# A gate product on rows without the norm: filling the seam between attention and the second MLP of a two-layer trunk

## The chip, the cores and the metric

The kernel runs on one core of a Trainium2 chip. The metric is the device time of one execution in microseconds (us). Times shown are medians of several executions; the profile comes from one execution of its own, whose time is given beside its span.

## The reference, cut to what matters

The trunk has two layers over 256 latent tokens (and 256 context tokens) of width 2048. What matters here is the end of layer 1: attention's output product, the norm in front of the MLP, and the MLP's first two products.

```python
h = h + ml[:, 2] * y_lat                       # y_lat = attention(...) @ w_o
u = modulate(rms_norm(h, norm2_g[i]), ml[:, 3], ml[:, 4])    # x * (1 + scale) + shift
gp = u @ w_gate                                # D_FF = 5504 = 43 column tiles of 128
gte = conv of width 3 over tokens (gp) + conv_b
h = h + ml[:, 5] * ((silu(gte) * (u @ w_up)) @ w_down)
return rms_norm(h, final_norm_g)
```

`rms_norm` multiplies a token's row by one number, rstd = (mean of squares + eps) ** -0.5. With the norm's gain and (1 + scale) folded into one factor M per channel, u = h * M * rstd + shift. So u @ w = rstd * ((h * M) @ w) + shift @ w, where rstd belongs to the token and shift @ w to the output channel.

## The kernel before

Channels lie on partitions: `hl` is 16 tiles (k = 0 to 15) of 128 channels by 256 tokens. Every product is in float32r, with weights and rows each split in a high part (a cast on ACT, line 148, `activation` or copy for rows) and a low part (value minus high part, a subtraction on DVE or POOL, line 150 for weights). A column tile of a layer-1 MLP product is 16 matmuls with the high weights against high and low rows side by side (512 columns, line 1018) and 16 with the low weights against the high rows (256 columns, line 1021).

Weights come in tiles of 128 x 1024 (512 KB) through the SP queue (line 132) into six staging rooms; `split` turns a room into a pair of tiles `wh`, `wl` out of a rotation of pools: `whp` with three pairs and, in the MLP of layer 1, `whx1` with three more. A room is free again when its low part is made. `turn` says whose turn it is in the rotation, and `hold` is a list of instructions behind which the next splits are queued on their engines (`tc.issue_after`, an order on one engine, not a semaphore). The order of the instructions on every engine is otherwise set by a planner that runs through the program with its own durations and takes the ready instruction that stands first in the program; `tc.high_priority()` puts instructions ahead.

The seam runs as follows. Attention's output product makes `op` for m = 0 to 15, with `wo` weights (lines 1351 to 1359); `o_end` (line 1363) adds it into `hl`. The fourth norm `n4` squares each row of `hl` on ACT (line 347), adds squares on DVE (line 353), and sums over channels on PE with columns of ones (line 366). The sums are reduced and scaled on DVE (lines 369, 370), raised to the power on POOL (374), spread over a diagonal on DVE (380) and broadcast by PE into the bank `n4b` (382), which is rstd. `norm_b` then makes the rows B[k]: DVE multiplies by M and rstd (986), ACT adds the shift and rounds (987), and the low part is made on DVE for even k (993) or by ACT and POOL for odd k (990, 991). `gu1(f)` makes the gate product `g` and the up product `u` of column tile f from B; `gate1(f)` evicts them (1029, 1030) and does convolution, SiLU and product. In `gu1(0)` the weights of both products of f = 0 are loaded and split ahead of the norm's rows, the second halves behind `tail`, the last `o_end`. In the trace these tiles are called `w_0h`, `w_0l` (first halves) and `w_1h`, `w_1l` (second halves); those of f = 1 are `wg_1h`, `wu_1h` and so on.

Of the kernel before, what the change touches and what calls it, by code (L numbers as in the profile page):

```python
# [60 lines left out]
def kernel(ctx: ExitStack, tc: tile.TileContext, xT, cxT, wmod, wg, wu, wd, wp,  # L61
                         wq, wv, wo, vec, cc, rope, inv, strips, out):
    nc = tc.nc
    main = ctx.enter_context(tc.tile_pool(name="main", bufs=1))
    wst = ctx.enter_context(tc.tile_pool(name="wst", bufs=3))
    whp = ctx.enter_context(tc.tile_pool(name="whp", bufs=3))
    ap0 = ctx.enter_context(tc.tile_pool(name="ap0", bufs=1))
# [12 lines left out]
    def flat(a):  # L80
        return a.rearrange("p s t -> p (s t)")
# [9 lines left out]
    ones = main.tile([P, P], F32, name="ones")  # L91
# [3 lines left out]
    ident = main.tile([P, P], F32, name="ident")  # L95
# [58 lines left out]
    def ld(src, name, share=0):  # L154
        return split(load(lambda a, b: src[:, a:b], 2048, name), name, share)
# [178 lines left out]
    class Norm:  # L334
# [8 lines left out]
        def add(self, h_of, k):  # L343
            sq = self.pool.tile([P, 512], F32, tag="t2", name=f"{self.name}q{k}")
            with self.urgent(k):
                for s in self.streams:
                    nc.scalar.activation(sq[:, T * s : T * s + T], h_of(s)[:, k, :], AF.Square)
# [11 lines left out]
        def totals(self):  # L359
            nj = self.n // P  # L360
            sqs = [self.acc] + self.last
            na = len(sqs)
            ps = bank("d", f"{self.name}s")
            for i, sq in enumerate(sqs):
                for j in range(nj):
                    nc.tensor.matmul(ps[:, na * j + i : na * j + i + 1], sq[:, P * j : P * j + P], ones[:, 0:1],
                                     start=True, stop=True)
# [8 lines left out]
        def spread(self, v, js, pb):  # L376

            dg = self.pool.tile([P, 512], F32, tag="t2", name=f"{self.name}d{js[0]}")
            for i, j in enumerate(js):
                nc.vector.tensor_scalar(dg[:, P * i : P * i + P], ident, v[:, j : j + 1], None, op0=ALU.mult)  # L380
# [63 lines left out]
    with ExitStack() as ph0:  # L444
# [6 lines left out]
        def h_of(s):  # L451
            return hc if s else hl
# [510 lines left out]

    for _ in moves:
        pass
    tail = _attention(tc, ap0, bank, ld, A, M, hl, wq, wv, wo, rope, band, ident, v_first)

    with ExitStack() as ph2:
        f1 = ph2.enter_context(tc.tile_pool(name="f1", bufs=8, reuse_waits="tile"))
        whx = ph2.enter_context(tc.tile_pool(name="whx1", bufs=3, reuse_waits="tile"))  # L970
        extra.extend([whx] * 3)

        def h_lat(s):
            return hl
# [1 line left out]
        n4 = Norm((0,), f1, "n4", 2)  # L976
        for k in range(KT):
            n4.add(h_lat, k)
        rstd = n4.each()[0]
        B = {}  # L980

        def norm_b(ks):
            for k in ks:
                a = ap0.tile([P, 2, 2, T], F32R, tag=f"A{k}", name=f"B{k}")[:, 0]
                y = f1.tile([P, 512], F32, tag="t2", name=f"nrmB{k}")[:, 0:T]
                nc.vector.scalar_tensor_tensor(y, hl[:, k, :], M(1, 4, k, 0), rstd[:, 0:T], op0=ALU.mult, op1=ALU.mult)
                nc.scalar.activation(a[:, 0], y, AF.Identity, bias=M(1, 3, k, 0))
                if k % 2:
                    z = f1.tile([P, 512], F32, tag="t2", name=f"nrmBz{k}")[:, 0:T]
                    nc.scalar.activation(z, y, AF.Identity, bias=M(1, 3, k, 0))  # L990
                    nc.gpsimd.tensor_tensor(a[:, 1], z, a[:, 0].bitcast(F32), op=ALU.subtract)
                else:
                    ins = nc.vector.scalar_tensor_tensor(a[:, 1], y, M(1, 3, k, 0), a[:, 0].bitcast(F32),
                                                         op0=ALU.add, op1=ALU.subtract)
                B[k] = a
                if k == 9:
                    hold[:] = [ins.ins]

        def gu1(f):
            res = []  # L1000
            pre = None
            if f == 0:
                pre = [load(lambda a, b: w[1, f][:, a:b], 2048, f"w{nm}1_{f}") for nm, w in (("g", wg), ("u", wu))]
                for q, ts in enumerate(pre):
                    first = split(ts[:1], f"w{q}1_{f}_0")
                    hold[:] = [tail]
                    pre[q] = first + split(ts[1:], f"w{q}1_{f}_1")
                    hold.clear()
                norm_b(range(KT))
            elif f == 2:  # L1010
                hold.clear()
            for q, (nm, wsrc) in enumerate((("g", wg), ("u", wu))):
                parts = pre[q] if pre else ld(wsrc[1, f], f"w{nm}1_{f}", 2 if f % 4 > 1 else 0)
                ps = bank("gu", f"{nm}1_{f}")
                for j, (hi, lo) in enumerate(parts):
                    for k in range(8 * j, 8 * j + 8):
                        c = P * (k % 8)
                        nc.tensor.matmul(ps, hi[:, c : c + P], flat(B[k]), start=(k == 0), stop=False)  # L1018
                    for k in range(8 * j, 8 * j + 8):
                        c = P * (k % 8)  # L1020
                        nc.tensor.matmul(ps[:, T:], lo[:, c : c + P], B[k][:, 0], start=False, stop=(k == KT - 1))  # L1021
                res.append(ps)
            return res

        def gate1(f, banks):
            res = []
            for nm, ps in zip("gu", banks):
                e = f1.tile([P, 512], F32, tag="t2", name=f"e{nm}_{f}")[:, 0:T]
                nc.scalar.copy(e, ps[:, T:])
                nc.vector.tensor_tensor(e, e, ps[:, :T], op=ALU.add)  # L1030
                res.append(e)
            pg, pu = res
            g1 = f1.tile([P, 512], F32, tag="t2", name=f"g1b_{f}")[:, 0:T]
            nc.scalar.activation(g1, pg, AF.Identity, scale=V("cw1_1")[:, f : f + 1], bias=V("cb_1")[:, f : f + 1])
            nc.vector.scalar_tensor_tensor(g1[:, 1:T], pg[:, 0 : T - 1], V("cw0_1")[:, f : f + 1],
                                           g1[:, 1:T], op0=ALU.mult, op1=ALU.add)
# [108 lines left out]
def _attention(tc, ap0, bank, ld, A, M, hl, wq, wv, wo, rope, band, ident, v_first):  # L1145
# [9 lines left out]
    with ExitStack() as es:  # L1155
# [179 lines left out]
                prev = v, P * j  # L1335
        queue.append(attend(KT - 1, *prev))

        X = {}

        def x_tile(k):  # L1340
            a = ap0.tile([P, 2, 2, T], F32R, tag=f"A{k}", name=f"oA{k}")[:, 0]
# [44 lines left out]
        for m in range(KT):  # L1386
# [9 lines left out]
        return ins  # L1396


# [97 lines left out]
```

## Time and profile before

| | |
|---|---|
| median of 3 runs | 3042.01 us (3039.23 to 3043.47) |
| the profiled execution | 3042.44 us, span 3040.7 us |
| PE busy | 2972.1 us (98% of the span) |
| DVE, ACT, POOL busy | 2054.5, 1347.4, 884.4 us |
| attention's last output tile ends on PE | 2293.9 us from the span's start |
| first product of the MLP of layer 1 starts | 2301.7 us |

The span is the time from the first to the last instruction of the profiled execution; the execution's own time is 1.7 us above it. All positions in the trace are us from the span's start.

### The profile page before, as it was taken

How to read it: one execution, taken by the hardware profiler on the slowest of the kernel's cores; microseconds unless marked ns; L12 is line 12 of the kernel's file. 1: busy time of each engine (PE TensorE's matmuls, PEld its weight loads, DVE VectorE, ACT ScalarE, POOL GpSimd, SP SyncE). 2: the span in 40 equal slices, each digit the busy share in tenths (PEclk: the TensorE clock that was granted, in tenths of full speed). 3: DMA queues.
4: the chain of work that ended last, by engine and by line, in shares of the span. 5: the costliest groups of instructions: out<-in, count | busy, mean ns of one | idle time of the engine just before them, and what ended most of it. 6: DMA issues, size and time to landing. Idle time of an engine off the chain costs nothing.

```text
span 3040.7 us, 40895 instructions
## 1 busy us (share of the span) xinstructions
PE 2972.1 (98%) x14846; PEld 2399.2 (79%) x14846; DVE 2054.5 (68%) x2894; ACT 1347.4 (44%) x2205; POOL 884.4 (29%) x868
## 2 busy tenths in 40 slices
PE   6999999999999999999999999999999999999998
PEld 2565678887888888888887888888888888888887
DVE  5445887576876867587686666474867666666666
ACT  3333473323334232333334444343546666566665
POOL 1111320303213030322413111010102566566665
PEclk9999999999999999999999999999999999999999
DMA  9878635454866857676783333333355555555563
GB/s 376 326 279 322 218 97 171 157 185 157 254 195 193 260 174 243 201 235 205 215 240 101 112 109 109 103 113 104 112 165 181 180 192 191 192 181 189 183 195 113
DMA packets 224778, 572.31 MB, mean 188 GB/s; under 512 B 55232, under 2 KB 68032, under 8 KB 224576
## 3 DMA queue, kind: packets, MB, share of 16 engines
q1 hardware_dynamic: 224576, 569.70, 58.0%
q8 instruction: 117, 1.92, 0.3%
q14 instruction: 85, 0.70, 0.1%
HBM read 563.32 MB, written 11.53 MB: 189 GB/s over the span
## 4 chain that ended last, share of the span: by engine, by line
PE 89%; issue 3%; DVE 3%; DMA 2%; ACT 1%; POOL 1%; SPq 0%; DVEq 0%; ACTq 0%; POOLq 0%
PE g L1018 5%; PE u L1018 5%; PE d L900 5%; PE d L902 5%; PE d L901 5%; PE d L1068 4%; PE u L865 4%; PE u L863 4%; PE u L864 4%; PE g L865 4%; PE g L864 4%; PE g L863 4%; PE u L1021 3%; PE g L1021 3%; PE d L1072 2%
## 5 line engine op out<-in xcount | busy, mean ns | idle before, releaser
L921 POOL TENSOR_TENSOR hl<-hl,dy 128x256 f32<-128x256 f32 x144 | 146.2, 1015 | 941.8 <-ACT dy L918 676.8
L1085 POOL TENSOR_TENSOR hl<-hl,dy 128x256 f32<-128x256 f32 x320 | 327.1, 1057 | 188.5 <-ACT dy L1083 186.2
L270 DVE SCALAR_TENSOR_TENSOR macc<-wm,sc,macc 128x512 f32<-128x512 f32 x360 | 262.3, 780 | 9.0 <-DMA wm<-wmod 8.9
L248 DVE SCALAR_TENSOR_TENSOR macc<-wm,sc,macc 128x1024 f32<-128x1024 f32 x120 | 160.4, 1336 | 87.3 <-DMA wm<-wmod 86.1
L918 ACT ACTIVATE dy<-d,modT 128x256 f32<-128x256 f32 x224 | 93.6, 471 | 138.6 <-PE d L902 134.7
L921 POOL TENSOR_TENSOR hc<-hc,dy 128x256 f32<-128x256 f32 x144 | 141.4, 982 | 0.0
L1261 POOL COPY bias<-rows 128x160 f32<-128x160 f32 x64 | 37.1, 579 | 306.2 <-issue 195.6
L1083 ACT ACTIVATE dy<-d,modT 128x512 f32<-128x512 f32 x160 | 104.5, 684 | 42.8 <-PE d L1072 41.3
L184 PE MATMUL mod<-wm,sc 128*32 128x512 f32 x640 | 101.6, 616 | 21.2 <-DVE n1q L353 18.9
L150 DVE TENSOR_TENSOR wd_2l<-wd,wd_2h 128x1024 fp32r<-128x1024 f32 (+1 forms) x44 | 58.6, 1343 | 60.5 <-ACT wd_2h L148 60.5
L488 ACT ACTIVATE sg<-g 128x512 f32<-128x512 f32 x43 | 27.3, 634 | 146.0 <-DVE g L485 145.9
L150 DVE TENSOR_TENSOR wd_3l<-wd,wd_3h 128x1024 fp32r<-128x1024 f32 (+1 forms) x44 | 54.5, 1262 | 52.7 <-ACT wd_3h L148 52.7
L575 POOL TENSOR_TENSOR pf<-ws,inv 128x256 f32<-128x256 f32 x32 | 27.9, 894 | 204.4 <-DVE ws L567 131.9
L148 ACT CAST wd_0h<-wd 128x1024 fp32r<-128x1024 f32 (+1 forms) x44 | 45.3, 1032 | 79.5 <-PE g L864 51.0
L150 DVE TENSOR_TENSOR wd_1l<-wd,wd_1h 128x1024 fp32r<-128x1024 f32 (+1 forms) x44 | 55.3, 1259 | 31.6 <-ACT wd_1h L148 31.6
L184 PEld LDWEIGHTS mod<-wm,sc 128*32 128x32 f32 x640 | 18.4, 109 | 65.1 <-issue 32.7
L1044 DVE TENSOR_TENSOR actb<-sgb,actb 128x256 fp32r<-128x256 f32 x43 | 52.9, 1229 | 23.7 <-ACT actb L1043 23.7
L900 PE MATMUL d<-act,wd_0h 128*128 128x512 f32 x172 | 67.4, 395 | 1.0 <-ACT dy L918 1.0
L900 PE MATMUL d<-act,wd_3h 128*128 128x512 f32 x172 | 68.2, 396 | 0.0
L901 PE MATMUL d<-act,wd_2h 128*128 128x512 f32 x172 | 68.1, 396 | 0.0
L150 DVE TENSOR_TENSOR wd_0l<-wd,wd_0h 128x1024 fp32r<-128x1024 f32 (+1 forms) x44 | 53.8, 1226 | 21.0 <-ACT wd_0h L148 21.0
L902 PE MATMUL d<-act,wd_0l 128*128 128x512 f32 x172 | 67.9, 395 | 0.0
(1708 smaller groups left out, 9381.7 us busy)
## 6 DMA issues: line engine op xcount, KB each, us to landing
wm<-wmod SPq DMA_DIRECT2D x384, 512.0 KB, 6.2
wd<-wd SPq DMA_DIRECT2D x168, 512.0 KB, 4.5
wg<-wg SPq DMA_DIRECT2D x156, 512.0 KB, 4.6
wu<-wu SPq DMA_DIRECT2D x156, 512.0 KB, 4.5
wv<-wv SPq DMA_DIRECT2D x32, 512.0 KB, 3.7
wk<-wq SPq DMA_DIRECT2D x32, 512.0 KB, 3.7
wq<-wq SPq DMA_DIRECT2D x32, 512.0 KB, 3.7
wo<-wo SPq DMA_DIRECT2D x32, 512.0 KB, 4.4
```

The source lines that it names most:

```text
L150: eng.tensor_tensor(lo[:, :n], t[:, :n], hi[:, :n].bitcast(F32), op=ALU.subtract)
L270: nc.vector.scalar_tensor_tensor(acc[:, s], w, sc2[:, k, s : s + 1], acc[:, s], op0=ALU.mult, op1=ALU.add)
L863: nc.tensor.matmul(ps, hi[:, c : c + P], xh, start=(k == 0), stop=False)
L864: nc.tensor.matmul(ps, hi[:, c : c + P], xl, start=False, stop=False)
L865: nc.tensor.matmul(ps, lo[:, c : c + P], xh, start=False, stop=(k == KT - 1))
L900: nc.tensor.matmul(ps, hi[:, o : o + P], xh, start=(i == 0), stop=False)
L901: nc.tensor.matmul(ps, hi[:, o : o + P], xl, start=False, stop=False)
L902: nc.tensor.matmul(ps, lo[:, o : o + P], xh, start=False, stop=(i == n - 1))
L921: nc.gpsimd.tensor_tensor(h_of(s)[:, k, :], h_of(s)[:, k, :], y[:, s], op=ALU.add)
L1018: nc.tensor.matmul(ps, hi[:, c : c + P], flat(B[k]), start=(k == 0), stop=False)
L1021: nc.tensor.matmul(ps[:, T:], lo[:, c : c + P], B[k][:, 0], start=False, stop=(k == KT - 1))
L1085: nc.gpsimd.tensor_tensor(hl[:, k, :], hl[:, k, :], y[:, q], op=ALU.add)
```

## The change

The gate product of f = 0 no longer reads the rows B but raw rows: high and low part of hl * M, made per k by one ACT and one DVE instruction behind the squares of the norm. They lie in the second half of the tile whose first half holds attention's rows `oA` and later B. `gate1(0)` multiplies that product by rstd and adds `gsh`, the shift times the weights, for which 32 more matmuls of two columns are made (`shift_sums`: 16 k by high and low weights), evicted by one reduction. On PE the low-weight matmuls of this product and the 32 sums are queued behind the last matmul of the norm's sums; the high-weight matmuls are not.

`whx1` has five pairs of tiles rather than three, so eight are in rotation, and `turn` is set so that the first five splits take the pairs of `whx1`. Early splits are both halves of `g` and `u` of f = 0 and the first half of `g` of f = 1, then, held, the second half of that (behind `tail`, the last square and the diagonal), and the two halves of `u` of f = 1 (behind the last square on ACT; on DVE behind the low parts of B[4] and of B[8]). Later splits are held behind the low part of B[12] until f = 3; before they were held behind that of k = 9 (in its place on DVE, that of k = 8) until f = 2.

```diff
-    tail = _attention(tc, ap0, bank, ld, A, M, hl, wq, wv, wo, rope, band, ident, v_first)
+    tail, rows = _attention(tc, ap0, bank, ld, A, M, hl, wq, wv, wo, rope, band, ident, v_first)
...
-        whx = ph2.enter_context(tc.tile_pool(name="whx1", bufs=3, reuse_waits="tile"))
-        extra.extend([whx] * 3)
+        whx = ph2.enter_context(tc.tile_pool(name="whx1", bufs=5, reuse_waits="tile"))
+        extra.extend([whx] * 5)
+        turn[0] += 2 - turn[0] % 8
...
+        raw = {}
+        for k in range(KT):
+            a = raw[k] = rows[k][:, 1]
+            with n4.urgent(k):
+                nc.scalar.activation(a[:, 0], hl[:, k, :], AF.Copy, scale=M(1, 4, k, 0))
+                nc.vector.scalar_tensor_tensor(a[:, 1], hl[:, k, :], M(1, 4, k, 0), a[:, 0].bitcast(F32),
+                                               op0=ALU.mult, op1=ALU.subtract)
+        sh = f1.tile([P, KT, 2], F32R, bufs=1, name="sh")
+        for k in range(0, KT, 4):
+            v = modT[1, 12 + k // 4][:, :, 0]
+            nc.scalar.copy(sh[:, k : k + 4, 0], v)
+            nc.vector.tensor_tensor(sh[:, k : k + 4, 1], v, sh[:, k : k + 4, 0].bitcast(F32), op=ALU.subtract)
         rstd = n4.each()[0]
...
-                a = ap0.tile([P, 2, 2, T], F32R, tag=f"A{k}", name=f"B{k}")[:, 0]
+                a = rows[k][:, 0]
...
             if f == 0:
-                pre = [load(lambda a, b: w[1, f][:, a:b], 2048, f"w{nm}1_{f}") for nm, w in (("g", wg), ("u", wu))]
-                for q, ts in enumerate(pre):
-                    first = split(ts[:1], f"w{q}1_{f}_0")
-                    hold[:] = [tail]
-                    pre[q] = first + split(ts[1:], f"w{q}1_{f}_1")
-                    hold.clear()
+                for nm, w in (("g", wg), ("u", wu)):
+                    early[0, nm] = ld(w[1, 0], f"w{nm}1_0")
+                ts = ask(1, "g", wg)
+                part(ts, 0, 1, "g")
+                part(ts, 1, 1, "g", tail, n4.done, n4.diag)
+                ps = bank("gu", "g1_0")
+                gu_b(ps, early[0, "g"], raw, n4.last_sum)
+                shift_sums(early[0, "g"], n4.last_sum)
+                res.append(ps)
                 norm_b(range(KT))
-            elif f == 2:
+                ts = ask(1, "u", wu)
+                part(ts, 0, 1, "u", n4.done, at[4])
+                part(ts, 1, 1, "u", n4.done, at[8])
+                hold[:] = [at[12]]
+            elif f == 3:
                 hold.clear()
...
+        def gu_b(ps, parts, x, behind=None):
+            for j, (hi, lo) in enumerate(parts):
+                for k in range(8 * j, 8 * j + 8):
+                    c = P * (k % 8)
+                    nc.tensor.matmul(ps, hi[:, c : c + P], flat(x[k]), start=(k == 0), stop=False)
+                with tc.issue_after(behind) if behind else ExitStack():
                     for k in range(8 * j, 8 * j + 8):
                         c = P * (k % 8)
+                        nc.tensor.matmul(ps[:, T:], lo[:, c : c + P], x[k][:, 0], start=False, stop=(k == KT - 1))
+        def shift_sums(parts, behind):
+            ps = bank("d", "gsh")
+            with tc.issue_after(behind):
+                for k in range(KT):
+                    c = P * (k % 8)
+                    for j, w in enumerate(parts[k // 8]):
+                        nc.tensor.matmul(ps[:, 0:2], w[:, c : c + P], sh[:, k, :], start=(k == 0 and j == 0),
+                                         stop=(k == KT - 1 and j == 1))
+            nc.vector.tensor_reduce(out=gsh, in_=ps[:, 0:2], axis=AX.X, op=ALU.add)
...
+                if f == 0 and nm == "g":
+                    nc.vector.tensor_tensor(e, e, rstd[:, 0:T], op=ALU.mult)
+                    nc.vector.tensor_scalar(e, e, gsh, None, op0=ALU.add)
```

## Rows read from the trace of the kernel before

**Rows 1.** The page: the span, then each engine's busy time.

```profile
span 3040.7 us, 40895 instructions
...
PE 2972.1 (98%) x14846; PEld 2399.2 (79%) x14846; DVE 2054.5 (68%) x2894; ACT 1347.4 (44%) x2205; POOL 884.4 (29%) x868
```

**Rows 2.** PE's waits from 2302 us to the end: total us, times, longest.

```profile
PE g L1018 <- DVE B L993: 2.2, 1, 2.2
PE n5b L382 <- DVE n5d L380: 1.8, 1, 1.8
```

**Rows 3.** The timeline of PE at the seam: start, us; in brackets idle before, releaser.

```profile
2293.57 0.28 PE L1353 MATMUL op<-oA,wo15l 128*128 128x256 f32 x1
2295.23 0.67 PE L366 MATMUL n4s<-ones,n4q 128*128 128x1 f32 x4 [1.38 <-ACT n4q L347]
2298.26 1.22 PE L382 MATMUL n4b<-n4d,ones 128*128 128x256 f32 x2 [2.37 <-DVE n4d L380]
2301.72 0.76 PE L1018 MATMUL g<-B,w_0h 128*128 128x512 f32 x1 [2.24 <-DVE B L993]
...
2305.70 0.48 PE L1018 MATMUL g<-B,w_0h 128*128 128x512 f32 x1
...
2326.02 2.00 PE L1018 MATMUL g<-B,wg_2h 128*128 128x512 f32 x8
```

**Rows 4.** Busy us by stretch: length, PE, PEld, DVE, ACT, POOL; clock, DMA share, GB/s.

```profile
2264.52:2286.75 22.23, 22.23 (x130) 19.55 (x128) 13.96 (x19) 10.41 (x13) 0.00 (x0) 1.00 0.60 183
...
2295.60:2295.80 0.20, 0.20 (x3) 0.20 (x2) 0.20 (x1) 0.00 (x0) 0.00 (x0) 0.58 0.00 0
...
2305.80:2306.00 0.20, 0.20 (x2) 0.18 (x1) 0.20 (x2) 0.20 (x1) 0.00 (x0) 0.82 0.00 0
...
2326.02:2337.19 11.17, 11.17 (x66) 9.83 (x65) 8.80 (x12) 7.40 (x14) 4.15 (x2) 1.00 0.56 181
```

**Rows 5.** The timeline of the seam on ACT and on POOL, one row of each.

```profile
2294.76 0.41 ACT L347 ACTIVATE n4q<-hl 128x256 f32<-128x256 f32 x1
...
2297.00 0.70 POOL L374 TENSOR_TENSOR n4v<-n4v,minus_half 128x2 f32<-128x2 f32 x1 [91.48 <-DVE n4v L370]
```

**Rows 6.** The timeline of the seam on DVE.

```profile
2293.89 0.48 DVE L1363 SCALAR_TENSOR_TENSOR hl<-op,modT,hl 128x256 f32<-128x256 f32 x1 [3.51 <-PE op L1353]
2294.29 1.22 DVE L150 TENSOR_TENSOR w_1l<-wg,w_1h 128x1024 fp32r<-128x1024 f32 x1
...
2296.55 0.16 DVE L369 TENSOR_REDUCE n4v<-n4s 128x2 f32<-128x6 f32 x1
...
2297.73 0.48 DVE L380 TENSOR_SCALAR n4d<-ident,n4v 128x128 f32<-128x128 f32 x2 [0.81 <-POOL n4v L374]
2299.52 1.66 DVE L986 SCALAR_TENSOR_TENSOR nrmB<-hl,modT,n4b 128x256 f32<-128x256 f32 x4 [1.31 <-PE n4b L382]
...
2320.14 1.23 DVE L150 TENSOR_TENSOR wu_1l<-wu,wu_1h 128x1024 fp32r<-128x1024 f32 x1 [5.66 <-ACT wu_1h L148]
```

**Rows 7.** Groups by line, 2293.69 to 2326.02 us: count, busy us, mean ns, idle before.

```profile
L986 DVE SCALAR_TENSOR_TENSOR nrmB<-hl,modT,n4b 128x256 f32<-128x256 f32 x16 | 6.9, 475 | 1.3 <-PE n4b L382 1.3
...
L993 DVE SCALAR_TENSOR_TENSOR B<-nrmB,modT,B 128x256 fp32r<-128x256 f32 x8 | 4.7, 589 | 0.0
```

**Rows 8.** The timeline of PE at the second and third norms.

```profile
357.10 1.12 PE L382 MATMUL n2b<-n2d,ones 128*128 128x512 f32 x2 [1.27 <-DVE n2d L380]
357.66 0.79 PE L742 MATMUL cg<-Ad,wcg_0h 128*128 128x512 f32 x1
...
1661.55 2.83 PE L366 MATMUL n3s<-ones,n3q 128*128 128x1 f32 x24
```

**Rows 9.** Busy us by stretch within the third norm's sums.

```profile
1664.00:1664.20 0.20, 0.20 (x4) 0.20 (x3) 0.00 (x0) 0.00 (x0) 0.00 (x0) 0.92 0.00 0
1664.20:1664.40 0.20, 0.17 (x2) 0.08 (x1) 0.00 (x0) 0.00 (x0) 0.00 (x0) 0.50 0.00 0
```

**Rows 10.** Waits of the SP queue, 2240 to 2350 us: total us, times, longest.

```profile
SPq L132 <- DVE wg_1l L150: 11.2, 2, 10.4
```

More of the change, by code (lines that the diff above doesn't have):

```diff
@@ L346, in add @@
                 for s in self.streams:
-                    nc.scalar.activation(sq[:, T * s : T * s + T], h_of(s)[:, k, :], AF.Square)
+                    self.done = nc.scalar.activation(sq[:, T * s : T * s + T], h_of(s)[:, k, :], AF.Square).ins
                 if k >= KT - self.ends:
@@ L365, in totals @@
                 for j in range(nj):
-                    nc.tensor.matmul(ps[:, na * j + i : na * j + i + 1], sq[:, P * j : P * j + P], ones[:, 0:1],
-                                     start=True, stop=True)
+                    ins = nc.tensor.matmul(ps[:, na * j + i : na * j + i + 1], sq[:, P * j : P * j + P], ones[:, 0:1],
+                                           start=True, stop=True)
+            self.last_sum = ins.ins
             v = main.tile([P, 4], F32, name=f"{self.name}v")[:, :nj]
@@ L379, in spread @@
             for i, j in enumerate(js):
-                nc.vector.tensor_scalar(dg[:, P * i : P * i + P], ident, v[:, j : j + 1], None, op0=ALU.mult)
+                self.diag = nc.vector.tensor_scalar(dg[:, P * i : P * i + P], ident, v[:, j : j + 1], None, op0=ALU.mult).ins
             n = P * len(js)
@@ L994, in norm_b, with ask @@
                                                          op0=ALU.add, op1=ALU.subtract)
+                    at[k] = ins.ins
                 B[k] = a
-                if k == 9:
-                    hold[:] = [ins.ins]
         def gu1(f):
             res = []
-            pre = None
             if f == 0:
-                pre = [load(lambda a, b: w[1, f][:, a:b], 2048, f"w{nm}1_{f}") for nm, w in (("g", wg), ("u", wu))]
-                for q, ts in enumerate(pre):
-                    first = split(ts[:1], f"w{q}1_{f}_0")
-                    hold[:] = [tail]
-                    pre[q] = first + split(ts[1:], f"w{q}1_{f}_1")
-                    hold.clear()
-                norm_b(range(KT))
-            elif f == 2:
+                def ask(e, nm, w):
+                    return load(lambda a, b: w[1, e][:, a:b], 2048, f"w{nm}1_{e}")
@@ new lines, in part @@
+                def part(ts, j, e, nm, *behind):
+                    hold[:] = behind
+                    early.setdefault((e, nm), []).extend(split(ts[j : j + 1], f"w{nm}1_{e}_{j}"))
+                    hold.clear()
+                for nm, w in (("g", wg), ("u", wu)):
[4 more added lines that the diff above has]
+                ps = bank("gu", "g1_0")
@@ L1011, in gu1 @@
+                gu_b(ps, early[0, "g"], raw, n4.last_sum)
+                shift_sums(early[0, "g"], n4.last_sum)
+                res.append(ps)
+                norm_b(range(KT))
+                ts = ask(1, "u", wu)
[3 more added lines that the diff above has]
+            elif f == 3:
                 hold.clear()
             for q, (nm, wsrc) in enumerate((("g", wg), ("u", wu))):
-                parts = pre[q] if pre else ld(wsrc[1, f], f"w{nm}1_{f}", 2 if f % 4 > 1 else 0)
+                if f == 0 and q == 0:
+                    continue
+                parts = early.pop((f, nm)) if (f, nm) in early else ld(wsrc[1, f], f"w{nm}1_{f}", 2 if f % 4 > 1 else 0)
@@ L1014, in gu1 @@
                 ps = bank("gu", f"{nm}1_{f}")
-                for j, (hi, lo) in enumerate(parts):
+                gu_b(ps, parts, B)
+                res.append(ps)
+            return res
+        def gu_b(ps, parts, x, behind=None):
[4 more added lines that the diff above has]
+                with tc.issue_after(behind) if behind else ExitStack():
@@ L1016, in gu1 @@
                     for k in range(8 * j, 8 * j + 8):
                         c = P * (k % 8)
[L1018 to L1023, printed above, removed]
+                        nc.tensor.matmul(ps[:, T:], lo[:, c : c + P], x[k][:, 0], start=False, stop=(k == KT - 1))
@@ new lines @@
+        early, at = {}, {}
+        gsh = main.tile([P, 1], F32, name="gsh")
+        def shift_sums(parts, behind):
[7 more added lines that the diff above has]
+            nc.vector.tensor_reduce(out=gsh, in_=ps[:, 0:2], axis=AX.X, op=ALU.add)
@@ L1336, in _attention @@
         queue.append(attend(KT - 1, *prev))
-        X = {}
+        X, rows = {}, {}
         def x_tile(k):
-            a = ap0.tile([P, 2, 2, T], F32R, tag=f"A{k}", name=f"oA{k}")[:, 0]
+            rows[k] = ap0.tile([P, 2, 2, T], F32R, tag=f"A{k}", name=f"oA{k}")
+            a = rows[k][:, 0]
             nc.scalar.copy(a[:, 0], O[k])
@@ L1395, in _attention @@
                 ins = o_end(ps, m)
-        return ins
+        return ins, rows
 def _cm(v):
```

## The prediction

> **What bounds the kernel now.** I read the page first, then PE's waits over the last quarter, then the timeline of PE at the seam, then DVE, ACT and POOL at the same place. The page shows PE busy for 98% of the span [rows 1], so a gain has to come from PE idling, from its clock, or from less PE work. From 2302 us to the end PE waits for nothing until the final norm [rows 2]: the first of those rows is the seam's own last wait, the second lies in the last 15 us. So after the seam whatever PE gains or loses is carried unchanged to the end, and the change can act at the seam alone. More weight tiles cannot shorten a stretch in which PE never waits.
>
> At the seam the last matmul of attention's output starts at 2293.57 us. Then PE waits three times: 1.38 us for the last square, 2.37 us for the diagonal, 2.24 us for the first low part of B, 5.99 us together [rows 3]. The chain in between reads: `o_end` at 2293.89 on DVE, the square at 2294.76 on ACT, the last sums at 2295.23 on PE, the reduction at 2296.55 on DVE, the power at 2297.00 on POOL, the diagonal at 2297.73, the broadcast at 2298.26, B from 2299.52 [rows 3, 5, 6]. [...] At 2326.02 the product of f = 2 begins with PE full: that is the mark for the sum.
>
> **The sum, term by term.** From 2293.7 to the mark are 32.3 us [rows 3]. What must be done in it at full clock: the four products of f = 0 and 1, which cost as much as the two of f = 2, twice, so 2 x 11.17 = 22.3 us [rows 4]; four last sums at 2.83 / 24 = 0.118 us, 0.5 us; the broadcast, at most the 0.56 us from the start of the second norm's twice as wide one to the next instruction [rows 8]. Together 23.4 us; 8.9 us are to be had at most. They are the 6.0 us of waits; 1.7 us of half clock on the first ten matmuls of B, which take 2301.72 to 2305.70, 3.98 us [rows 3]; at full clock half a product takes 11.17 / 4 = 2.79 us, of which its eight 512-column matmuls are two thirds of the columns, 1.86 us, so ten take 2.3 us [rows 4]; the rest, 1.2 us, is the start of each burst and half clock on the sums and the broadcast.
>
> **The raw product as filling.** It is moved, not added: a quarter of 22.3, 5.6 us, that no longer waits for rstd. The high half, 16 matmuls and 3.7 us, may start at 2293.7; the low half and the 32 sums come behind the norm's last sum. With the 32 sums there are 9.4 us of filling for 6.0 us of waits, so the gap is covered, and PE reaches work on B at about 2293.7 + 9.4 + 1.0 = 2304.1 us, when B has been arriving since 2301.
>
> **The 32 sums** are the only new PE work. Nearest row: one-column sums with 128 x 128 weights, 0.118 us each [rows 8], hence 3.8 us. That row is fp32, the new ones are float32r, one instruction per product too; I take it as it is. Lower bound: two columns alone cost next to nothing beside 256, so 0 us, if the weight loads were hidden; upper bound: twice, 7.6 us, if all run at half clock. So 8.9 - 3.8 = 5.1 us remain.
>
> **The clock.** [...] In the third norm, full-width products end at 1661.55, 24 sums of one column follow without a break, and the clock falls at about 1664.2, during the sums, PE busy throughout [rows 8, 9]. Here 32 sums follow each other for 3.8 us, longer than that run of 2.83 us. I take a fall, at the end of the sums, with the price of the first ten matmuls of B above, 1.7 us: 5.1 - 1.7 = 3.4 us. Bounds: nothing, or 3.6 us if the sums too slow down by half their number.
>
> [...]
>
> **The raw rows** cost 16 x 0.41 us on ACT (the square's row) and 16 x 0.48 us on DVE (`o_end`'s row) [rows 5, 6], 6.6 and 7.7 us. All but the last are ready before the seam: in the last 22.2 us of full output tiles DVE is free for 8.3 and ACT for 11.8 us [rows 4], enough for all 16 rows beside two of the three further splits, and there are twice as many tiles before these; I cost them at nothing. Without that cover they would stand in the norm's chain (rival 2). Only k = 15 comes late, one instruction on each engine, less than the 1.22 us split of `w_1l` that stands between the last `o_end` and the reduction now [rows 6], of which there are two and which now are made earlier. The further early splits, 1.22 us each on DVE, take the place of these and of DVE's 3.51 us of waiting for the last `op` [rows 6].
>
> **Held splits.** The second half of `g` of f = 1 is queued behind the last square and the diagonal: DVE's 1.31 us of waiting for the broadcast [rows 6] holds its 1.22 us; behind it are the rows of B, which wait for the broadcast anyway. `u` of f = 1 comes behind the low parts of B[4] and B[8]: 2.4 us in front of the later rows of B, where three such splits stood before. DVE makes B in 6.9 + 4.7 = 11.6 us [rows 7], with 2.4 us 14.0, so B[15] comes at about 2313.5. PE at 2304.1 has `u` and `g` with their first halves, 5.6 us, then that of `u` of f = 1, 2.8 us, then second halves: it needs B[15] after 2315. Hidden, by about 2 us. Behind B[12], at about 2311, wait the splits of f = 2, needed at about 2321; DVE idled 5.66 us there behind a cast of `wu_1` [rows 6], so it has the room. Loads are as many as before; on SP the room of `wg_1` held the queue up to 10.4 us [rows 10], and is now free some 8 us earlier. The eight small instructions for `sh`, the reduction and two more DVE instructions in `gate1(0)`, 0.5 us each at most, lie in the same idle time: nothing.
>
> **Order on PE.** PE takes what the planner put in order. If it expects the last square or the diagonal too early, PE stands at the sums or the broadcast though filling lies behind them. Bounds 0 and 3.75 us (the first two waits in full); I take 0.5 us, near the lower end, since high-half matmuls are free to stand on either side of the sums and two kinds of filling stand on either side of the broadcast. So 3.4 - 0.5 = 2.9 us.
>
> **Forecast.** 3042.4 (the profiled execution's own time) - 2.9 = 3039.5 us; the median shown is 0.4 us lower, so 3039.1 us as a median.
>
> **Rival 1: the clock stays.** The raw product and B's product lie close enough on both sides of the sums. Then 1.7 us more: 3037.4 us. For it: at the second norm PE waited 1.27 us ahead of the broadcast and still did its twice as wide one in 0.56 us [rows 8], so no fall there. Against: the third norm.
>
> **Rival 2, the other sign: raw rows in the norm's chain.** Place: DVE between the last `o_end` (2293.89) and the diagonal (2297.73). If the planner leaves the raw rows to the end, up to 7.7 us of DVE work delay the diagonal and with it B, from 2301.7 to 2309.4; filling ends at 2304.1, PE idles 5.3 us, and the clock falls: 5.1 - 5.3 - 1.7 = -1.9, 3043.9 us. It decides from a delay of about 5.8 us (12 rows). For it: they stand behind the squares in the program. Against: DVE's 8.3 free us in 22.2, and the squares themselves ran as soon as `hl` was ready.
>
> **Rival 3: the change does not do what it says.** The tiles of `g` are not split when the output product ends (the low part of the second half is made at 2294.29 now [rows 6]), or the raw product is put behind the broadcast. Then the waits stay and the sums are added: 3042.0 + 3.8 = 3045.8 us. Against: the first five splits have tiles of their own.
>
> **Rival 4: the sums cost little.** At half price, 1.9 us, and with the clock kept: 3035.5 us.
>
> **Chances.** About 0.2% (6.1 us) is what a measurement of this kernel tells from no change: 3035.9 and 3048.1 us. Forecast 0.50, rival 1 0.24, rival 2 0.10, rival 3 0.05, rival 4 0.06, anything else 0.05. The range from 3035.6 to 3043.4 us leaves out rivals 3 and 4 in the main, the worse part of rival 2 and some of the rest. All cases but rival 4 and the unknown lie within 0.2%: faster 0.09, same 0.86, slower 0.05.
>
> **What would show it.** Right: the three waits of PE gone or below 1 us together; 16 matmuls of the raw product starting within 0.3 us of 2293.7; 32 matmuls of two columns about 0.12 us apart; a clock of 0.5 for some 4 us behind them; the product of f = 2 some 3 us earlier than 2326.0; no PE wait after it. Wrong: PE waiting for B behind the sums, raw rows on DVE after 2294, sums apart by another figure, or PE waits later than 2326, where splits held behind B[12] would come late.

## The result and the profile after

The changed kernel takes 3046.89 us as a median of 21 runs, the kernel before 3043.14 us in 21 runs on the same chip; the ratio is 1.0015 with an interval of 1.0009 to 1.0021. So the change costs 0.15%: 3.75 us between the medians, 2.7 to 6.4 us by the interval. The forecast was 3039.1 us, a gain of 2.9 us: the sign was wrong, and the time lies above the range.

The page of the kernel after (the span, the busy times), to be set beside [rows 1]:

```profile
span 3043.3 us, 40973 instructions
...
PE 2973.8 (98%) x14878; PEld 2398.9 (79%) x14878; DVE 2038.5 (67%) x2917; ACT 1353.8 (44%) x2225; POOL 879.2 (29%) x868
```

PE has 32 instructions and 1.7 us of busy time more; of PE the page says no more than that. PE's waits from 2286 us to the end, after (total us, times, longest), beside [rows 2]:

```profile
PE g L1053 <- DVE eg L1078: 5.3, 1, 5.3
PE n5b L383 <- DVE n5d L381: 1.8, 1, 1.8
PE u L1053 <- POOL oA L1005: 0.9, 2, 0.8
PE u L1053 <- DVE oA L1007: 0.6, 1, 0.6
PE n4s L366 <- ACT n4q L347: 0.2, 1, 0.2
```

The waits for the diagonal and the first low part of B are gone, and that for the last square has shrunk to 0.2 us. A wait of 5.3 us has come: the gate product of f = 2 waits for `eg`, the eviction of that of f = 0, because both use one PSUM bank. The timeline of PE after, beside [rows 3]:

```profile
2289.46 0.28 PE L1405 MATMUL op<-oA,wo15l 128*128 128x256 f32 x1
2289.58 1.31 PE L1053 MATMUL g<-oA,wg_0h 128*128 128x512 f32 x5
...
2291.96 0.61 PE L366 MATMUL n4s<-ones,n4q 128*128 128x1 f32 x4 [0.16 <-ACT n4q L347]
...
2299.96 0.25 PE L1069 MATMUL gsh<-sh,wg_0h 128*128 128x2 f32 x1
2300.07 0.25 PE L1069 MATMUL gsh<-sh,wg_0l 128*128 128x2 f32 x1
2300.18 0.48 PE L1053 MATMUL u<-oA,wu_0h 128*128 128x512 f32 x1
...
2320.18 3.75 PE L1053 MATMUL g<-oA,wg_2h 128*128 128x512 f32 x8 [5.28 <-DVE eg L1078]
...
2331.17 0.40 PE L1053 MATMUL u<-oA,wu_1h 128*128 128x512 f32 x1
...
2339.18 2.03 PE L1053 MATMUL g<-oA,wg_3h 128*128 128x512 f32 x8
```

The raw product starts 0.12 us behind the last `op` matmul and the sums are 0.11 us apart, as forecast. Then PE, in its fixed order, comes to `g` of f = 2 and stands; the last matmuls of f = 0 and f = 1 (from 2326.95 on, that of 2331.17 among them) are queued behind it. I call the stretch from the last `op` matmul to the first of `g` of f = 3 the seam. It lasts 2337.19 - 2293.57 = 43.62 us before [rows 3, 4] and 2339.18 - 2289.46 = 49.72 us after, 6.1 us longer. (The absolute times differ for another reason: over the profiles of this study the last `op` matmul starts anywhere from 2285.9 to 2297.9 us, with the same order on PE up to the output product. So seams are compared, not positions.)

What follows the seam takes 702.6 to 704.6 us in all thirteen profiles, so a longer seam reaches the end; the output product ahead of it, from its first matmul to its last, takes 104.1 to 106.7 us over them, 106.2 before and 104.5 after. So 6.1 us of seam and 2.7 to 6.4 us of time agree.

Windows of the seam after (length, busy us of PE, PEld, DVE, ACT, POOL, clock, DMA share, GB/s), beside [rows 4]:

```profile
2289.46:2339.18 49.72, 42.70 (x236) 36.02 (x235) 35.44 (x51) 27.98 (x49) 19.74 (x13) 0.90 0.43 142
2315.60:2315.80 0.20, 0.00 (x0) 0.00 (x0) 0.20 (x1) 0.00 (x0) 0.20 (x1) 1.00 0.00 0
2315.80:2316.00 0.20, 0.00 (x0) 0.00 (x0) 0.20 (x1) 0.00 (x0) 0.20 (x1) 0.84 0.00 0
2315.90:2326.00 10.10, 5.82 (x18) 4.98 (x19) 5.17 (x6) 1.04 (x1) 3.52 (x2) 0.50 0.61 208
```

The granted clock did not fall at the sums (1.00 from 2289.46 to 2315.6). It fell from 1.00 to 0.50 at about 2315.9, inside the 5.28 us wait, and the first 5.82 us of work behind it ran at that half clock; taken as half speed, that is 2.9 us lost. So the 6.1 us come out like this: waits of 0.16 + 0.19 + 0.75 + 0.65 + 5.28 = 7.03 us where 5.99 stood, +1.0; sums 32 x 0.111 = +3.6; half clock 2.9 us against 2.8 before (5.59 us busy of 10.2 at a clock of 0.50, from about 2295.7 to 2305.8), +0.1. Of the 1.4 us left, 0.36 are four sums of the norm that now stand inside the seam (2290.73; before, at 2292.18, ahead of it); about 1 us remains that I can put nowhere.

Why `eg` is late stands in the rows of DVE, POOL and ACT after, beside [rows 6, 7]:

```profile
2308.81 2.54 DVE L1007 SCALAR_TENSOR_TENSOR oA<-nrmB,modT,oA 128x256 fp32r<-128x256 f32 x1
2311.26 0.86 DVE L1000 SCALAR_TENSOR_TENSOR nrmB<-hl,modT,n4b 128x256 f32<-128x256 f32 x2
2312.05 1.83 DVE L1007 SCALAR_TENSOR_TENSOR oA<-nrmB,modT,oA 128x256 fp32r<-128x256 f32 x1
2313.80 1.75 DVE L150 TENSOR_TENSOR wg_2l<-wg,wg_2h 128x1024 fp32r<-128x1024 f32 x1
2315.48 1.74 DVE L150 TENSOR_TENSOR wu_2l<-wu,wu_2h 128x1024 fp32r<-128x1024 f32 x1
2317.14 2.56 DVE L1007 SCALAR_TENSOR_TENSOR oA<-nrmB,modT,oA 128x256 fp32r<-128x256 f32 x1
2319.62 0.41 DVE L1078 TENSOR_TENSOR eg<-eg,g 128x256 f32<-128x256 f32 x1
```

```profile
2308.66 2.40 POOL L150 TENSOR_TENSOR wg_2l<-wg,wg_2h 128x1024 fp32r<-128x1024 f32 x1
2311.02 2.58 POOL L150 TENSOR_TENSOR wu_2l<-wu,wu_2h 128x1024 fp32r<-128x1024 f32 x1
2313.57 2.58 POOL L1005 TENSOR_TENSOR oA<-nrmBz,oA 128x256 fp32r<-128x256 f32 x2
2316.10 3.32 POOL L150 TENSOR_TENSOR wg_3l<-wg,wg_3h 128x1024 fp32r<-128x1024 f32 x1
```

```profile
2312.99 0.35 ACT L1077 COPY eg<-g 128x256 f32<-128x256 f32 x1
```

The splits of f = 2 are held behind B[12]'s low part, but that part is made on DVE, and an order on one engine holds nothing on POOL. So POOL makes two of them (2308.66 to 2313.60) ahead of its low parts of B[13] and B[15]. DVE's own instructions lengthen meanwhile: the low part of B (L1007), 0.48 us when undisturbed, takes 2.54, 1.83 and 2.56 us, and each time ends 0.28 or 0.29 us behind the end of the POOL split that it overlaps (2311.35 behind 2311.06, 2313.88 behind 2313.60, 2319.70 behind 2319.42). The third of these splits is one of f = 3 (2316.10), which nothing holds on POOL either. The excess of the five lengthened rows from 2308.81 to 2317.14 over 0.48 and 1.22 us is 2.06 + 1.35 + 0.53 + 0.52 + 2.08 = 6.5 us, more than PE's 5.28 us, and the eviction stands behind them in DVE's queue, though ACT's half of it was done at 2313.3.

### The profile page after: what moved, and what is told of

It reads as the page before. It is cut to its first block, busy times and chain, and to the rows that moved or that the text cites. A ratio compares the mean times of both kernels' runs of the same rounds, so it can differ in the third digit from the quotient of the medians.

```text
span 3043.3 us, 40973 instructions
## 1 busy us (share of the span) xinstructions
PE 2973.8 (98%) x14878; PEld 2398.9 (79%) x14878; DVE 2038.5 (67%) x2917; ACT 1353.8 (44%) x2225; POOL 879.2 (29%) x868
## 4 chain that ended last, share of the span: by engine, by line
PE 90%; DVE 5%; DMA 2%; issue 2%; ACT 1%; POOL 0%; SPq 0%; DVEq 0%; ACTq 0%; POOLq 0%
PE g L1053 5%; PE u L1053 5%; PE d L901 5%; PE d L903 5%; PE d L902 5%; PE d L1119 5%; PE u L866 4%; PE u L864 4%; PE u L865 4%; PE g L866 4%; PE g L865 4%; PE g L864 4%; PE g L1057 3%; PE u L1057 3%; PE d L1123 2%; PE mod L184 2%
## 5 line engine op out<-in xcount | busy, mean ns | idle before, releaser
L922 POOL TENSOR_TENSOR hl<-hl,dy 128x256 f32<-128x256 f32 x144 | 143.5, 996 | 941.6 <-ACT dy L919 678.1
L1136 POOL TENSOR_TENSOR hl<-hl,dy 128x256 f32<-128x256 f32 x320 | 313.0, 1009 | 234.8 <-ACT dy L1134 231.9
L1134 ACT ACTIVATE dy<-d,modT 128x512 f32<-128x512 f32 x160 | 104.5, 684 | 57.5 <-PE d L1123 57.2
L148 ACT CAST wd_1h<-wd 128x1024 fp32r<-128x1024 f32 (+1 forms) x44 | 45.0, 1026 | 56.1 <-PE u L1053 29.7
L903 PE MATMUL d<-act,wd_1l 128*128 128x512 f32 x172 | 67.7, 394 | 0.9 <-DVE wd_1l L150 0.9
```

Of the source, the lines that this page charges most:

```text
L903: nc.tensor.matmul(ps, lo[:, o : o + P], xh, start=False, stop=(i == n - 1))
L922: nc.gpsimd.tensor_tensor(h_of(s)[:, k, :], h_of(s)[:, k, :], y[:, s], op=ALU.add)
L1136: nc.gpsimd.tensor_tensor(hl[:, k, :], hl[:, k, :], y[:, q], op=ALU.add)
```

## The experiments

**Theory A:** POOL's splits of f = 2, which nothing holds, run ahead of the last low parts of B and slow DVE; without them the seam falls to near what the sum of the prediction gives. **Theory B:** the eviction of the first gate product is queued too late on DVE, whatever POOL does; an early eviction frees the bank and cures it. **Theory C:** the sums cost more than they fill. Times come from 5 rounds beside runs of the kernel before on the same chip (medians of 3044.02 us for the first four kernels below, 3042.72 for the next four, 3043.15 for the last three). A ratio's interval is about 0.0009 to either side, 2.7 us. The last three columns are from each kernel's one profile. The spans of these profiles differ by up to 18.7 us (3049.9 us in `hold_dve`, 3031.2 in `hold_pool`): 11.9 of them lie ahead of the seam, where the last `op` matmul starts at 2297.85 and at 2285.94, and 6.8 in it. The planner also sets PE's order anew with each edit: in `hold` and `hold_pool` it puts `g` of f = 2 behind all matmuls of f = 0 and f = 1, in `evict` and `both` it spreads it among them.

| kernel | median us | ratio [95%] | seam us | PE waits in the seam, us | us at half clock |
|---|---|---|---|---|---|
| before | 3043.14 | 1 | 43.6 | 2.4, 2.2, 1.4 | 10.2 |
| after | 3046.89 | 1.0015 [1.0009, 1.0021] | 49.7 | 5.3, 0.9, 0.6, 0.2 | 10.2 |
| hold | 3041.09 | 0.9991 [0.9982, 1.0] | 41.8 | none | 6.8 |
| evict | 3041.80 | 0.9994 [0.9986, 1.0003] | 44.7 | 1.8, 0.6 | 6.8 |
| nosums | 3046.88 | 1.0013 [1.0004, 1.0022] | 47.1 | 5.3, 2.4 | 10.2 |
| six | 3042.77 | 0.9998 [0.9988, 1.0007] | 43.0 | 0.4 | 6.8 |
| hold_dve | 3045.34 | 1.0011 [1.0003, 1.002] | 48.4 | 3.3, 0.2 | 13.7 |
| hold_pool | 3038.81 | 0.9990 [0.9982, 0.9999] | 41.7 | none | 6.8 |
| hold_mix | 3040.12 | 0.9993 [0.9985, 1.0002] | 40.6 | 1.1, 0.5 | 0 |
| eight | 3043.93 | 1.0004 [0.9995, 1.0013] | 44.9 | 3.9, 2.2, 1.0, 0.3 | 6.8 |
| hold_pool_mix | 3038.89 | 0.9989 [0.9980, 0.9998] | 40.2 | 1.1 | 0 |
| hold_nosums | 3038.78 | 0.9987 [0.9978, 0.9996] | 39.4 | 2.2, 0.2 | 3.4 |
| both | 3040.03 | 0.9989 [0.9981, 0.9998] | 42.1 | none | 6.8 |

**hold.** The later splits stand behind the last low part of B on each engine, POOL's too.

```diff
-                    nc.gpsimd.tensor_tensor(a[:, 1], z, a[:, 0].bitcast(F32), op=ALU.subtract)
+                    at[k] = nc.gpsimd.tensor_tensor(a[:, 1], z, a[:, 0].bitcast(F32), op=ALU.subtract).ins
...
-                hold[:] = [at[12]]
+                hold[:] = [at[14], at[15]]
```

> Splits from f = 2 on are held behind the low part of B[14] on DVE and of B[15] on POOL, not behind B[12]. Theory A (late rows: the splits of f = 2 run on POOL and DVE ahead of the last rows of B and of the eviction of the first gate product; PE then waits 5.3 us and runs at half clock for some 4 us): both go, 6 to 8 us less than the changed kernel, 3039 to 3041 us, ratio to before about 0.999. Theory B (bank order: PE takes the product of f = 2 before the rest of f = 0 and 1 and waits for a PSUM bank): the planner now puts that product last, so B expects the same here. Theory C (the 32 two-column sums, 3.6 us, are the loss): no change, 3046 us.

PE waits nowhere in the seam. It is 7.9 us shorter than after, and the ratio to the kernel before goes from 1.0015 to 0.9991. POOL now makes B[15]'s low part first (its timeline in `hold`):

```profile
2315.71 1.56 POOL L1005 TENSOR_TENSOR oA<-nrmBz,oA 128x256 fp32r<-128x256 f32 x1 [0.46 <-ACT nrmBz L1004]
2317.23 3.38 POOL L150 TENSOR_TENSOR wg_2l<-wg,wg_2h 128x1024 fp32r<-128x1024 f32 x1
```

The groups of DVE's rows of B by line (count, busy us, mean ns, idle before), first in the kernel after from 2289.46 to 2326 us, then in `hold` from 2293 to 2330 us:

```profile
L1007 DVE SCALAR_TENSOR_TENSOR oA<-nrmB,modT,oA 128x256 fp32r<-128x256 f32 x8 | 9.7, 1209 | 0.0
L1000 DVE SCALAR_TENSOR_TENSOR nrmB<-hl,modT,n4b 128x256 f32<-128x256 f32 x16 | 7.0, 473 | 2.3 <-PE n4b L383 2.2 <-POOL oA L1005 0.2
```

```profile
L1000 DVE SCALAR_TENSOR_TENSOR nrmB<-hl,modT,n4b 128x256 f32<-128x256 f32 x16 | 7.0, 474 | 2.1 <-PE n4b L383 2.1
L1007 DVE SCALAR_TENSOR_TENSOR oA<-nrmB,modT,oA 128x256 fp32r<-128x256 f32 x8 | 4.2, 525 | 1.9 <-ACT oA L1001 1.8
```

L1007 falls from 9.7 to 4.2 us, 5.5 us; L1000 stays at 7.0. L1007 reads two tiles from SBUF; one of L1000's operands, `n4b`, is a PSUM bank. Whether that makes the difference no run shows.

**evict.** `g` of f = 0 is evicted right behind its sums, ahead of the rows of B.

```diff
                 shift_sums(early[0, "g"], n4.last_sum)
                 res.append(ps)
+                e = f1.tile([P, 512], F32, tag="t2", name="eg_0")[:, 0:T]
+                nc.scalar.copy(e, ps[:, T:])
+                nc.vector.tensor_tensor(e, e, ps[:, :T], op=ALU.add)
+                out_early.append(e)
```

> The first gate product is evicted into SBUF before the rows of B are made, so its PSUM bank is free early; the splits are as in the changed kernel. Theory B: the wait of 5.3 us goes and with it the half clock, 3039 to 3041 us. Theory A: the last rows of B are still late, PE fills the wait only with some 4 us of the product of f = 2, so 3 to 4 us less than the changed kernel, 3043 us, and 1 to 2 us of waiting for rows of B. Theory C: 3046 us.

The wait for `eg` is gone, but PE waits 1.8 us for a low part of B on DVE, and the seam is still 2.9 us longer than in `hold`. On DVE the low part beside POOL's split is as long as it was:

```profile
2312.55 2.54 DVE L1007 SCALAR_TENSOR_TENSOR oA<-nrmB,modT,oA 128x256 fp32r<-128x256 f32 x1
```

So B names the place where the delay reaches PE, not its source. The gain is larger than A expected of this run, though: 0.9994 cannot be told from the 0.9991 of `hold`, so the early eviction hides most of the delay from PE.

**nosums.** The 32 sums and their reduction are replaced by a memset of `gsh`; this leaves the shift's part of the first gate product out.

```diff
-            ps = bank("d", "gsh")
...
-            nc.vector.tensor_reduce(out=gsh, in_=ps[:, 0:2], axis=AX.X, op=ALU.add)
+            nc.gpsimd.memset(gsh, 0.0)
```

> The 32 sums of shift times weights are left out (the shift's part of the first gate product is zero). Theory C: 3.6 us less than the changed kernel, 3043 us. Theories A and B: the end of the seam is set by DVE and POOL, PE waits as much longer as it has less to do, 3045 to 3047 us.

The kernel is no faster than the changed one, 1.0013 against 1.0015. PE's waits show why: the stall is as long, and the time saved ahead of it comes back as a wait for rows of B.

```profile
PE g L1053 <- DVE eg L1071: 5.3, 1, 5.3
PE u L1053 <- DVE oA L1007: 2.4, 2, 2.2
```

C falls as the cause of the loss.

**six.** The changed kernel with the three pairs of `whx1` that were there before.

```diff
-        whx = ph2.enter_context(tc.tile_pool(name="whx1", bufs=5, reuse_waits="tile"))
-        extra.extend([whx] * 5)
-        turn[0] += 2 - turn[0] % 8
+        whx = ph2.enter_context(tc.tile_pool(name="whx1", bufs=3, reuse_waits="tile"))
+        extra.extend([whx] * 3)
```

> The changed kernel with three pairs of tiles in the second pool, six in rotation, as before. Theory A: the splits of f = 2 find no tile until PE has used the early ones, so they can't run ahead of the last rows of B: the wait shrinks to 2 us or less, 3040 to 3042 us. Theory B: PE's order still has the product of f = 2 ahead of the rest, the wait for the bank stays, 3045 us or more. Theory C: 3046 us.

With six pairs no tile is free for the splits of f = 2 so early: POOL's first starts 22.3 us behind the last `op` matmul (2316.85 - 2294.55) where it was 19.2 (2308.66 - 2289.46). One low part of B is still slow (2.54 us at 2318.01), but `eg` is evicted by 2320.89, ahead of `g` of f = 2 at 2322.70, which here too stands ahead of the last matmuls of f = 0 and f = 1 (2327.16). So that order on PE makes no stall by itself, and B's expectation for this run falls. The stall is gone, the seam is 43.0 us, and the time is that of the kernel before.

**eight.** The reverse: the kernel before with five pairs of `whx1` and the line on `turn`.

> The kernel before with only the tiles of the change: five pairs in the second pool, the turn set, its own first product on rows with the norm. Theory A: more tiles alone let splits run early, but the three waits at the norm stay; the last rows of B can be late here too; 0 to 3 us more than before, ratio 1.000 to 1.001. Rival (tiles are harmless, the loss needs the raw product): 1.000.

No difference that can be told (1.0004; both expectations allow it), and no wait for `eg`, though this one seam is 1.2 us longer than before, with 3.9 us of waiting for the diagonal where 2.4 stood. So the five pairs alone make no such stall, and by `six` the raw product makes none without them; the stall needs both.

**hold_dve** holds DVE alone (`hold[:] = [at[14]]`), **hold_pool** POOL alone (`hold[:] = [at[12], at[15]]`, with B[15]'s low part on POOL).

> Longer hold on DVE alone (behind B[14]); the splits on POOL as in the changed kernel. Theory A1 (DVE's two splits ahead of B[14] are what is late): PE's wait falls to under 1.5 us, 3041 us. Theory A2 (POOL's splits ahead of B[13] and B[15], and DVE's longer durations beside them, are): the wait stays at 4 us or more, 3045 us.

> Longer hold on POOL alone (behind B[15]); DVE's splits wait for B[12] as in the changed kernel. Theory A2: PE's wait falls to under 1.5 us, 3041 us. Theory A1: B[14] stays behind two splits on DVE, PE waits 2 to 4 us, 3044 us.

`hold_pool` does all that `hold` does (0.9990 against 0.9991, no wait); `hold_dve` does little (1.0011, and a wait of 3.3 us, between its two expectations and nearer A2's). Its timelines, POOL's rows first, then DVE's:

```profile
2321.19 2.59 POOL L150 TENSOR_TENSOR wg_2l<-wg,wg_2h 128x1024 fp32r<-128x1024 f32 x1
2323.74 3.33 POOL L150 TENSOR_TENSOR wu_2l<-wu,wu_2h 128x1024 fp32r<-128x1024 f32 x1
2327.03 1.70 POOL L1005 TENSOR_TENSOR oA<-nrmBz,oA 128x256 fp32r<-128x256 f32 x1
```

```profile
2321.44 3.42 DVE L150 TENSOR_TENSOR wg_2l<-wg,wg_2h 128x1024 fp32r<-128x1024 f32 x1
2324.79 3.37 DVE L150 TENSOR_TENSOR wu_2l<-wu,wu_2h 128x1024 fp32r<-128x1024 f32 x1
2328.08 0.41 DVE L1078 TENSOR_TENSOR eg<-eg,g 128x256 f32<-128x256 f32 x1
```

DVE's splits now stand behind its rows of B, but POOL's still run ahead of B[15]. Beside them DVE's take 3.4 us each instead of 1.22, and the eviction behind them is late again: 3.3 us of waiting.

In `hold_pool` POOL's edit also moved `g` of f = 2 on PE. Rows of PE, DVE and POOL there:

```profile
2316.35 2.03 PE L1053 MATMUL g<-oA,wg_2h 128*128 128x512 f32 x8
2310.15 0.41 DVE L1078 TENSOR_TENSOR eg<-eg,g 128x256 f32<-128x256 f32 x1
2311.05 2.28 DVE L1081 TENSOR_SCALAR eg<-eg,gsh 128x256 f32<-128x256 f32 x1
2310.78 2.39 POOL L150 TENSOR_TENSOR wg_2l<-wg,wg_2h 128x1024 fp32r<-128x1024 f32 x1
```

The eviction ends 24.6 us behind the last `op` matmul (2310.56 - 2285.94), in the changed kernel 30.6 us (2320.03 - 2289.46). PE came to `g` of f = 2 there after 25.4 us, when its wait began (2314.90). So with POOL held the bank is free in time for either order.

**both** is `hold` and `evict` in one kernel.

> This run evicts the first gate product early and holds the splits of f = 2 (both cures). Theory A (one chain: POOL's splits make the last rows of B late, and those make the eviction late): with the splits held the early eviction has nothing left to win, a seam of 41 to 42.5 us as in hold, and a median within 2 us of hold's (3041.1 us). Rival (two independent losses): the gains add up, 6.1 + 5.0 us off the changed kernel's 49.7 us seam, under 40 us.

42.1 us of seam, as `hold` alone (41.8): the gains do not add up, so it is one chain.

**hold_mix** and **hold_pool_mix** spread the sums, one or two at a time, between the raw product's matmuls, on top of `hold` and of `hold_pool`.

```diff
+            for j, (hi, lo) in enumerate(parts):
+                for k in range(8 * j, 8 * j + 8):
+                    c = P * (k % 8)
+                    with tc.issue_after(behind) if j else ExitStack():
+                        nc.tensor.matmul(ps, hi[:, c : c + P], flat(raw[k]), start=(k == 0), stop=False)
+                        if j:
+                            sums(2)
+                with tc.issue_after(behind):
+                    for k in range(8 * j, 8 * j + 8):
+                        c = P * (k % 8)
+                        nc.tensor.matmul(ps[:, T:], lo[:, c : c + P], raw[k][:, 0], start=False, stop=(k == KT - 1))
+                        sums(1)
```

> The kernel with the longer hold on both engines, and the 32 sums mixed one or two at a time between the matmuls of the raw product behind the norm's last sum, not in one run after it. Theory D (what is left of the loss in the longer hold is the clock, which fell inside the run of sums and cost some 3.4 us): no fall, or a later one, 3 us less than the longer hold alone, 3038 us, ratio about 0.998. Rival (the fall follows from the light work as a whole, whatever its order): the same as the longer hold, 0.999.

> This run holds the splits of f = 2 on POOL behind POOL's low part of k = 15 (on DVE behind that of k = 12, as in the changed kernel) and spreads the 32 sums one or two at a time between the raw product's matmuls. Theory A (POOL's unheld splits are the whole of the loss, and the price left is the fall of the clock in the run of sums): no wait for eg, no stretch at half clock, the seam from the last output matmul to the product of f = 3 at about 41.7 - 3.4 = 38.3 us, and a median some 4 us below the kernel before, ratio 0.9985 to 0.999. Rival (the spread sums cost what the fall cost, because each sits between two full matmuls with its own weights): a seam of 40.5 us or more as in hold_mix, and a ratio of 0.999 as in hold_pool.

In both the granted clock stays at 1.00 through the whole seam; that of `hold_pool_mix`:

```profile
2294.41:2334.64 40.23, 39.06 (x236) 34.07 (x235) 32.92 (x50) 26.74 (x48) 20.63 (x13) 1.00 0.46 147
```

Against `hold_pool` 6.8 us at half clock are gone, by half speed 3.4 us of time, but the seam is only 1.4 us shorter: 1.1 us come back as a wait for POOL's rows of B, which PE now reaches sooner, and 0.9 us I cannot place. In time the two cannot be told apart (0.9989 and 0.9990). So the clock was kept, but not the time that was expected with it: 40.2 us is nearer the rival's 40.5 us than 38.3 us.

**hold_nosums** is `hold` without the sums (the shift's part left out again).

> This run holds the splits of f = 2 as hold does and leaves out the shift's part of the first gate product (a memset stands for the 32 sums). With the late rows gone, it prices the sums on the path. If the sums cost 3.6 us plus the fall of the clock behind them (3.4 us), as in the prediction's sum, the waits that they filled may come back in part: filling without the sums is 5.6 us for 6.0 us of waits, so the seam comes to about 41.8 - 3.6 - 3.4 + 0.5 to 3 = 35.5 to 38 us and the time 4 to 6 us below that of hold. Rival (the sums fill a wait that would be there anyhow): a seam within 1.5 us of hold's 41.8 us, with a PE wait for the rows of B of 2 us or more, and no difference in time.

The seam is 2.4 us shorter than in `hold`, between the two expectations: 2.4 us of waits come back for the 3.6 us of sums, and half clock is 3.4 us rather than 6.8. The clock falls without the sums too, 0.7 us behind the wait of 2.2 us (at 2305.07; in `nosums` inside such a wait). In time, 0.9987 against 0.9991 is within the intervals. So the sums cost about 2 us of seam net, the clock included; the rest of their time would be waiting.

The best of the versions that compute everything are `hold_pool` and `hold_pool_mix`: 0.9990 and 0.9989, by the ratios some 3 us below the kernel before and 7 to 8 us below the changed one.

## Why the prediction was wrong

**The step that failed is "Held splits"**, the sentence that behind B[12] the splits of f = 2 wait and that DVE "has the room". It took one order for both engines. POOL's half of these splits was held by nothing, and eight pairs of tiles let it start at 2308.66, where B[13] and B[15] were still to be made. And it took DVE's durations as fixed, at 14.0 us for all of B and two splits of `u`; the two splits of f = 2 that this order lets stand ahead of B[14] on DVE (2313.80 and 2315.48) are not in them. In the kernel after, the low parts alone grew by 5.5 us over `hold`. The last row was forecast for 2313.5; B[14] was ready at 2319.70, in a seam that began 4.1 us earlier, so 10 us late, against a margin of "about 2 us". `hold_pool` shows that POOL's part of this step carries the loss: that edit alone turns 1.0015 into 0.9990, and 0.0010 of 3042 us is 3.0 us, against the 2.9 us forecast. How well the two figures agree is luck: the interval runs from 0.3 to 5.5 us, and with what was measured for the other terms the sum gives 8.9 - 3.6 (sums) - 3.4 (clock) = 1.9 us, which is what the seam of `hold_pool` gained (43.6 - 41.7).

The nearest sign that the prediction named ("PE waits later than 2326, where splits held behind B[12] would come late") looks the other way: the splits came early, the rows of B came late, and PE stood from 2314.9 to 2320.2. It had no price either. Late rows belonged among the rivals, with the eviction of `g` as the instruction that is late next.

**Filling:** right. 5.99 us of waits became 0.16 us up to the first product of B, and the raw product started at once.

**The sums:** right in size, 0.111 us each for 0.118. `hold_nosums` shows that only some 2 us of their 3.6 would be saved.

**The clock:** in the changed kernel itself it kept through the sums and fell in the stall, so the fall that was forecast did not come there. In the other six profiles with the sums in one run, but for the broadcast that stands in it (`hold`, `evict`, `six`, `hold_dve`, `hold_pool`, `both`) it came inside that run, with PE busy, and a clock of 0.50 followed for about 6.8 us, by half speed 3.4 us, twice what was taken. In `hold`: windows before and after the fall, and the sums on either side.

```profile
2302.00:2302.20 0.20, 0.20 (x4) 0.20 (x3) 0.20 (x2) 0.20 (x2) 0.00 (x0) 1.00 0.00 0
2302.40:2302.60 0.20, 0.20 (x2) 0.20 (x2) 0.20 (x2) 0.20 (x2) 0.00 (x0) 0.50 0.00 0
```

```profile
2302.03 0.25 PE L1069 MATMUL gsh<-sh,wg_0h 128*128 128x2 f32 x1
2302.14 0.25 PE L1069 MATMUL gsh<-sh,wg_0l 128*128 128x2 f32 x1
2302.25 0.35 PE L1069 MATMUL gsh<-sh,wg_0h 128*128 128x2 f32 x1
2302.46 0.35 PE L1069 MATMUL gsh<-sh,wg_0l 128*128 128x2 f32 x1
```

It lasts 6.8 us and PE is busy throughout, so it costs 3.4 us where 1.7 were taken. The clock thus fell both with PE idle (the changed kernel, inside the 5.28 us wait) and with PE busy (`hold`, behind a stretch without a wait, and the third norm [rows 9]). What makes it fall no run isolates, nor how close to the sums the products would have to lie for rival 1.

**Raw rows (rival 2):** hidden, as forecast. The last one ran on DVE at 2292.34, and the reduction followed at 2292.74, behind PE's sums at 2291.96. Rival 2 had the right sign and the wrong place. Rival 3 gave the nearest time, 3045.8 us, but it falls: the change does what it says, and its waits are gone. Rivals 1 and 4 did not come about either: the clock was lost elsewhere, and the sums cost what they were forecast to.

**Order on PE:** taken at 0.5 us for places ahead of B, where 0.16 us of waiting came. It mattered elsewhere: the planner put `g` of f = 2 ahead of the last rows of f = 0 and f = 1, and so the late eviction became a stall. In another order PE would have come to B[14] instead, which was ready only at 2319.70, while the stall ended at 2320.18; that is an estimate from the rows of the changed kernel. What the two would cost apart was not measured.

## What to carry to other kernels

When splits or loads are allowed earlier, follow each engine's queue by itself: an order that names an instruction of one engine leaves the same work on the others free to run ahead. Where DVE and POOL work side by side on tiles in SBUF, take DVE's durations from rows beside a busy POOL (the low part of B took 0.48 us undisturbed and up to 2.56 us beside a POOL split), and look for what stands behind the lengthened instructions in DVE's queue: here it was the eviction that frees a PSUM bank. Filling a gap on PE is worth its time only up to the next wait; that next one needs a price in the sum.

## What the runs showed of the hardware

Beside POOL's instructions, DVE's on tiles in SBUF became longer, and several of them ended soon behind the end of the POOL row that they overlapped. In the kernel after, three low parts, 0.48 us when undisturbed, ended 0.28 or 0.29 us behind the end of the POOL split that was already running, whether that left 2.54, 1.83 or 2.56 us. The DVE split of 2313.80, 1.75 us long where 1.22 is undisturbed, ended at 2315.55, 1.24 us behind the end of the first of POOL's two parts from 2313.57, if that took 0.74 us as at 2306.28; that end is an estimate. POOL's split of 2316.10 took 3.32 us where that of 2308.66 took 2.40, and ended 2.20 us behind the end of DVE's split at 2317.22. The instruction with an operand in PSUM (L1000) took 0.43 us each at 2311.26, during the POOL split of 2311.02. One with a single tile as input became longer too: the addition of `gsh` (L1081), 0.35 us in the kernel after at 2320.52, took 2.28 us in `hold_pool` at 2311.05, to 0.16 us behind the end of the POOL split of 2310.78. What makes the two engines lengthen each other's rows no run isolates.

In a run of two-column matmuls the granted clock fell from 1.00 to 0.50 without any pause on PE (`hold`, 2302.25, and five more of the seven profiles with that run), after which they came 0.214 us apart rather than 0.111. With the same number of them spread between wide matmuls it stayed at 1.00 (`hold_mix`, `hold_pool_mix`), in one profile each. In the changed kernel it did not fall in the run either; what decided between that profile and `hold` stays open.
